# Where weight parts start within 256 bytes: all of them at 64 or 192, and the tiles behind the sinks' 128 bytes further on

## The chip, the cores and the metric

The kernel runs on one core of one Trainium2 chip. The metric is device time in microseconds (us) of one execution. The kernel before took 1211.8 us, the median of 3 runs (1211.75 to 1212.57).

TensorE (PE in the profile, PEld for its weight loads) multiplies; VectorE (DVE) and ScalarE (ACT) do the elementwise work; GpSimd (POOL) does a little; SyncE (SP) issues most DMAs. SBUF is the memory on the chip that all of them read: 128 partitions, and in each of them a tile has a start address in bytes. "Place" in this document is that address modulo 256.

## What is computed

Two layers of a decoder trunk on 512 tokens of width 1024, in float32. Cut to the parts that matter here:

```python
for i in range(DEPTH):                                  # 2 layers
    h = _rms_norm(x, mix_norm[i])
    if i % 2 == 0:                                      # sliding-window attention and short convolution
        x = x + _attn_conv_mixer(h, cos, sin, hy_w_in[j], ..., hy_sinks[j], ..., hy_w_out[j])
    else:                                               # chunked gated linear attention
        x = x + _gla_mixer(h, gla_w_in[j], ..., gla_w_out[j])
    x = x + _conv_ffn(_rms_norm(x, ffn_norm[i]), ffn_w_up[i], ..., ffn_w_down[i])
    x = x + _per_layer_embedding(x, p[i], ple_norm[i], ple_w_gate[i], ple_w_proj[i])
```

Nearly all the arithmetic is in the products with the weights: `hy_w_in`, `hy_w_out`, `gla_w_in`, `gla_w_out`, `ple_w_gate`, `ple_w_proj`, and above all `ffn_w_up` (1024 x 5632) and `ffn_w_down` (2816 x 1024).

## The kernel before

**Split products.** A float32 value is cut into a high part, which ScalarE rounds to the type float32r, and a low part, which VectorE gets as the difference. A product of two such values is three matmuls: high x high, high x low, low x high (`mm3`, lines 162 to 168; the third line of the three, L168, has the low part of the stationary side). Weights arrive by DMA in tiles "raw" and are cut into tiles "wh" and "wl"; activations are cut into pairs "a", "b" (normed activations), "uh" and "ul" (the feed-forward's inner values), "yh" and "yl" (the mixers' outputs), "ph" and "pl" (the embedding).

**Two ways to cut weights.** `cut` makes plain parts; they serve `mm3`, mostly as the stationary operand (128 x 128), with 512 tokens moving. `cut_blocks` and `first_forms` make parts for `seven` (lines 875 to 877), which computes a 2 x 2 block product with seven products instead of eight; there 256 tokens move. The sums of activations that the seven products need lie in tiles "four" (and low parts beside them). `seven` serves the feed-forward's gate columns in the up-projection and some of the down-projection. In it `product` issues 4 x 3 = 12 matmuls: of the seven products, four have "four" as their moving side and three have plain activations. In `down` the rows of inner values come in sets A (8 to 13), B (0 to 7) and C (14 to 21); A and C are cut into "four" tiles, B into uh and ul.

**Roles.** In a few places the weights are the moving side and the activations the stationary one: the keys, values and queries of the first mixer, the values of the second, and the gate of the last embedding (`ple1`, lines 1372 to 1374 by its helper `add`). That gate also has some weight chunks in "four" tiles rather than wh and wl.

**Where tiles lie.** Tiles stand in pools, and a pool gives each tag its buffers one after the other, in the order of first use. The pools are laid out in this order: constants (cp), the residual (xp), activations a and b (fp), weights raw, wh, wl (wp), scratch (sp), small columns (sm), and behind them the pool of the running stage, which holds "four", the inputs, the attention's and the linear attention's tiles, "zt" and "z". Sizes up to the small columns are multiples of 256 bytes, so a, b, raw, wh and wl start at place 0. Tiles of wh and wl are 1088 elements wide (4352 bytes, 17 x 256), of which 1024 are used; `weight_tiles` says from which element on. `cut` takes element 0; `cut_blocks` and `first_forms` pass BLOCKS = (16, 48), so that wh starts 64 bytes and wl 192 bytes behind the tile's start. The small columns are 32 bytes each; among them is "sink", 16 elements (64 bytes). They end at place 128, and so all the tiles of the stage pools start at place 128.

**Order.** TensorE's order in the heavy stages is the program's (a manual schedule); the change leaves every engine's instructions in the order that they had.

Of the kernel before, what the change touches and what calls it, by code (L numbers as in the profile page):

```python
# [9 lines left out]
F32 = mybir.dt.float32  # L10
F32R = mybir.dt.float32r
# [7 lines left out]
P = 128  # L19
S = 512  # L20
# [6 lines left out]
NQ, NKV, HD = 8, 2, 64  # L27
# [27 lines left out]

BLOCKS = (16, 48)


class Kernel:
# [53 lines left out]
        self.nc.sync.dma_start(raw, src)  # L115
        return self.cut(raw, by)

    def weight_tiles(self, offs=(0, 0)):

        return [  # L120
            self.wp.tile([P, 1024 + 64], F32R, tag=g, name=self.nm(g), bufs=3)[:, o : o + 1024]
            for g, o in zip(("wh", "wl"), offs)
        ]

    def raw(self, na, nb):
# [303 lines left out]
    def mixer0(self):  # L429
        nc, a, tc = self.nc, self.a, self.tc  # L430
        with tc.tile_pool(name="m0", bufs=1) as mp:
# [62 lines left out]
            self.end_norm(sums=sums)  # L494
            with tc.issue_after(last[1].ins):
                C, Sn = self.rope_tables(mp)
            sink = self.sm.tile([P, 16], F32, name="sink", bufs=1)[:, :NQ]
            self.late(sink[:, :1])
            nc.gpsimd.dma_start(sink, a["hy_sinks"][0:1, :].partition_broadcast(P))
            nc.vector.tensor_scalar_mul(sink, sink, -1.0)  # L500
            h = HD // 2
# [310 lines left out]
    def cut_blocks(self, src, wide=True):  # L812

        nc = self.nc
        if wide:
            h, l = self.weight_tiles(BLOCKS)
        else:
            h, l = (
                self.sp.tile([P, S + 64], F32R, tag="sq", name=self.nm("t2"), bufs=2)[:, o : o + S] for o in BLOCKS
            )  # L820
        h, l = (x.rearrange("p (j n) -> p j n", n=src.shape[2]) for x in (h, l))
        nc.scalar.activation(h, src, AF.Copy)  # L822
        nc.vector.tensor_tensor(l, src, h.bitcast(F32), ALU.subtract)  # L823
        h, l = (x.rearrange("p j n -> p (j n)").rearrange("p (k n) -> p k n", n=P) for x in (h, l))
        n = 2 if wide else 1
        return lambda j, c: (h[:, n * j + c, :], l[:, n * j + c, :])
# [7 lines left out]
    def first_forms(self, ev, od, raw=None):  # L834

        nc = self.nc
        b11, b12, b21, b22 = ev[:, :, :P], ev[:, :, P:], od[:, :, :P], od[:, :, P:]
        if raw is not None:
            plain = self.cut_blocks(raw[:, :, :P])
        else:  # L840
            h, l = self.weight_tiles(BLOCKS)
            h, l = (x.rearrange("p (j u n) -> p j u n", u=2, n=P) for x in (h, l))
            for u, b in enumerate((b11, b21)):
                self.split((h[:, :, u], l[:, :, u]), b)
            plain = lambda j, c: (h[:, j, c], l[:, j, c])
        nc.vector.tensor_tensor(b11, b12, b11, ALU.subtract)
        nc.vector.tensor_tensor(b12, b22, b12, ALU.subtract)  # L847
        return plain
# [242 lines left out]
    def down(self, i, acts, forms, both, work, finish):  # L1091
# [76 lines left out]
        for t, p in enumerate(plan):  # L1168
            todo.append((1, lambda t=t: cut(t)))
            if p[4] is not None:  # L1170
                todo.append((1, lambda u=p[4]: first_forms(u)))
                todo.append((1, lambda u=p[4]: more_forms(u)))
# [804 lines left out]
```

## Time and profile before

| what | value |
| --- | --- |
| median of the runs | 1211.8 us (1211.75 to 1212.57) |
| the profiled execution, whole | 1211.79 us |
| its span in the profile | 1210.0 us |
| granted TensorE clock | 1.0 |
| instructions | 17728, of them 7018 matmuls and 7018 weight loads |
| HBM traffic | 114.37 MB read, 2.10 MB written |

How to read it: the page gives the busy time of each engine and its share of the span. A group of instructions has the line of the kernel, the engine, the operation, then output<-inputs by tile names, the shapes, the count, the busy time and the mean duration of one in ns. The timeline lists instructions by start time (first column, us) and duration (second column, us). Matmuls are pipelined: one starts well before the one ahead of it has ended, so the distance of two starts, not the duration, is what a matmul costs. The profile has no addresses; they come from the built program.

### The profile page before, as it was taken

How to read it: one execution, taken by the hardware profiler on the slowest of the kernel's cores; microseconds unless marked ns; L12 is line 12 of the kernel's file. 1: busy time of each engine (PE TensorE's matmuls, PEld its weight loads, DVE VectorE, ACT ScalarE, POOL GpSimd, SP SyncE). 2: the span in 40 equal slices, each digit the busy share in tenths (PEclk: the TensorE clock that was granted, in tenths of full speed). 3: DMA queues.
4: the chain of work that ended last, by engine and by line, in shares of the span. 5: the costliest groups of instructions: out<-in, count | busy, mean ns of one | idle time of the engine just before them, and what ended most of it. 6: DMA issues, size and time to landing. Idle time of an engine off the chain costs nothing.

```text
span 1210.0 us, 17728 instructions
## 1 busy us (share of the span) xinstructions
PE 1203.6 (99%) x7018; PEld 1042.1 (86%) x7018; DVE 969.4 (80%) x1543; ACT 667.9 (55%) x1093; POOL 44.7 (4%) x64
## 2 busy tenths in 40 slices
PE   9999999999999999999999999999999999999998
PEld 8877789999999889888988988889999999888887
DVE  6786687899989986746679876778999898978595
ACT  7466565656554643534563654555665555645374
POOL 2600000000000000000100000000000000000000
PEclk9999999999999999999999999999999999999999
DMA  7232222324242332232322212322232423322501
GB/s 221 76 101 70 73 70 77 133 71 139 71 139 70 127 114 86 92 105 80 111 93 69 77 64 71 104 87 88 88 123 70 140 70 131 122 87 100 206 1 70
DMA packets 111128, 117.61 MB, mean 97 GB/s; under 512 B 2841, under 2 KB 106323, under 8 KB 111045
## 3 DMA queue, kind: packets, MB, share of 16 engines
q1 hardware_dynamic: 109680, 115.35, 28.8%
q8 instruction: 55, 0.90, 0.3%
q0 software_dynamic: 560, 0.42, 0.2%
q10 hardware_dynamic: 804, 0.70, 0.2%
q14 instruction: 29, 0.23, 0.1%
HBM read 114.37 MB, written 2.10 MB: 96 GB/s over the span
## 4 chain that ended last, share of the span: by engine, by line
PE 95%; DVE 3%; ACT 1%; issue 0%; ACTq 0%
PE ps L166 14%; PE ps L167 14%; PE ps L168 14%; PE pa L167 7%; PE pa L166 7%; PE pa L168 7%; PE ps L875 6%; PE ps L876 6%; PE ps L877 6%; PE pa L875 2%; PE pa L876 2%; PE pa L877 2%; PE ps L1374 1%; PE ps L1373 1%; PE ps L1372 1%; DVE wl L147 1%
## 5 line engine op out<-in xcount | busy, mean ns | idle before, releaser
L146 ACT ACTIVATE wh<-raw 128x1024 fp32r<-128x1024 f32 (+4 forms) x154 | 152.4, 992 | 150.4 <-PE ps L167 103.2
L147 DVE TENSOR_TENSOR wl<-raw,wh 128x1024 fp32r<-128x1024 f32 (+4 forms) x154 | 175.1, 1138 | 56.4 <-ACT wh L146 55.6
L822 ACT ACTIVATE wh<-raw 128x1024 fp32r<-128x1024 f32 x78 | 82.7, 1061 | 124.0 <-DVE raw L847 65.8
L935 DVE SCALAR_TENSOR_TENSOR zt<-z,vfa,zt 128x510 f32<-128x510 f32 (+1 forms) x176 | 130.6, 744 | 11.7 <-ACT zt L933 11.2
L823 DVE TENSOR_TENSOR wl<-raw,wh 128x1024 fp32r<-128x1024 f32 x78 | 95.3, 1222 | 20.6 <-ACT wh L822 20.5
L933 ACT ACTIVATE zt<-z,vfb 128x512 f32<-128x512 f32 x88 | 71.0, 809 | 23.9 <-DVE four L986 12.8
L166 PE MATMUL ps<-b,wh 128*128 128x512 f32 x192 | 76.6, 399 | 0.0
L167 PE MATMUL ps<-b,wh 128*128 128x512 f32 x192 | 75.1, 391 | 0.0
L168 PE MATMUL ps<-b,wl 128*128 128x512 f32 x192 | 74.9, 390 | 0.0
L167 PE MATMUL pa<-a,wh 128*128 128x512 f32 x176 | 69.1, 392 | 0.0
L167 PE MATMUL pa<-b,wh 128*128 128x512 f32 x176 | 69.0, 392 | 0.0
L166 PE MATMUL pa<-a,wh 128*128 128x512 f32 x176 | 68.8, 391 | 0.0
L166 PE MATMUL pa<-b,wh 128*128 128x512 f32 x176 | 68.8, 391 | 0.0
L168 PE MATMUL pa<-a,wl 128*128 128x512 f32 x176 | 68.7, 390 | 0.0
L168 PE MATMUL pa<-b,wl 128*128 128x512 f32 x176 | 68.6, 390 | 0.0
L876 PE MATMUL ps<-four,wh 128*128 128x256 f32 x232 | 65.3, 281 | 0.0
L875 PE MATMUL ps<-four,wh 128*128 128x256 f32 x232 | 65.1, 281 | 0.0
L877 PE MATMUL ps<-four,wl 128*128 128x256 f32 x232 | 64.8, 279 | 0.0
L166 PE MATMUL ps<-a,wh 128*128 128x512 f32 x160 | 63.6, 398 | 0.0
L167 PE MATMUL ps<-a,wh 128*128 128x512 f32 x160 | 62.4, 390 | 0.0
L168 PE MATMUL ps<-a,wl 128*128 128x512 f32 x160 | 62.4, 390 | 0.0
L166 PE MATMUL ps<-uh,wh 128*128 128x512 f32 x128 | 50.2, 392 | 0.0
(472 smaller groups left out, 3500.6 us busy)
## 6 DMA issues: line engine op xcount, KB each, us to landing
raw<-in_ffn_w_up_dram SPq DMA_DIRECT2D x44, 1024.0 KB, 5.0
raw<-in_ffn_w_down_dram SPq DMA_DIRECT2D x13, 1024.0 KB, 4.7
raw<-in_hy_w_in_dram SPq DMA_DIRECT2D x8, 1024.0 KB, 4.9
raw<-in_gla_w_in_dram SPq DMA_DIRECT2D x8, 1024.0 KB, 5.0
raw<-in_ffn_w_down_dram SPq DMA_DIRECT2D x8, 768.0 KB, 4.1
raw<-in_ple_w_gate_dram SPq DMA_DIRECT2D x6, 1024.0 KB, 4.6
raw<-in_hy_w_out_dram SPq DMA_DIRECT2D x16, 256.0 KB, 4.0
raw<-in_gla_w_out_dram SPq DMA_DIRECT2D x4, 1024.0 KB, 4.6
```

Source lines behind the costliest of these rows:

```text
L146: nc.scalar.activation(hv, v, AF.Copy)
L147: nc.vector.tensor_tensor(lv, v, hv.bitcast(F32), ALU.subtract)
L166: mm(out, lh, rh, start=start, stop=False, **kw)
L167: mm(out, lh, rl, start=False, stop=False, **kw)
L168: mm(out, ll, rh, start=False, stop=stop, **kw)
L822: nc.scalar.activation(h, src, AF.Copy)
L823: nc.vector.tensor_tensor(l, src, h.bitcast(F32), ALU.subtract)
L875: mm(out, wh, xh, start=first and j == 0, stop=False, **kw)
L876: mm(out, wh, xl, start=False, stop=False, **kw)
L877: mm(out, wl, xh, start=False, stop=j == ND // 2 - 1, **kw)
L933: nc.scalar.activation(y, z, AF.Identity, scale=w2[:, f : f + 1], bias=bb[:, f : f + 1])
L935: nc.vector.scalar_tensor_tensor(out=y[:, tap:], in0=z[:, : S - tap], scalar=w[:, f : f + 1], in1=y[:, tap:], op0=ALU.mult, op1=ALU.add,)
```

## The change

Every pair of weight tiles now starts at elements (16, 48), those of `cut` and of `ple1` too; the constant has a new name and `weight_tiles` no argument. The tile "sink" is 48 elements wide instead of 16, of which the same 8 are used, so the small columns behind it and all tiles of the stage pools move by 128 bytes: the latter from place 128 to place 0. The tiles of a, b, u, y and raw stay where they were. No instruction is added, removed or moved, and no shape changes.

```diff
-BLOCKS = (16, 48)
+STARTS = (16, 48)
...
-    def weight_tiles(self, offs=(0, 0)):
+    def weight_tiles(self):
 
         return [
             self.wp.tile([P, 1024 + 64], F32R, tag=g, name=self.nm(g), bufs=3)[:, o : o + 1024]
-            for g, o in zip(("wh", "wl"), offs)
+            for g, o in zip(("wh", "wl"), STARTS)
         ]
...
-            sink = self.sm.tile([P, 16], F32, name="sink", bufs=1)[:, :NQ]
+            sink = self.sm.tile([P, 48], F32, name="sink", bufs=1)[:, :NQ]
...
         if wide:
-            h, l = self.weight_tiles(BLOCKS)
+            h, l = self.weight_tiles()
         else:
             h, l = (
-                self.sp.tile([P, S + 64], F32R, tag="sq", name=self.nm("t2"), bufs=2)[:, o : o + S] for o in BLOCKS
+                self.sp.tile([P, S + 64], F32R, tag="sq", name=self.nm("t2"), bufs=2)[:, o : o + S] for o in STARTS
             )
...
-            h, l = self.weight_tiles(BLOCKS)
+            h, l = self.weight_tiles()
```

## The prediction

> **What bounds the kernel now.** I read the page first, then the waits of TensorE, then its groups with shapes kept apart, and last the timeline of single matmuls, because the change alters no instruction, only where tiles lie.
>
> ```profile
> span 1210.0 us, 17728 instructions
> ...
> PE 1203.6 (99%) x7018; PEld 1042.1 (86%) x7018; DVE 969.4 (80%) x1543; ACT 667.9 (55%) x1093; POOL 44.7 (4%) x64
> ...
> PEclk9999999999999999999999999999999999999999
> ...
> PE 95%; DVE 3%; ACT 1%; issue 0%; ACTq 0%
> ```
>
> TensorE is busy in 1203.6 of 1210.0 us, at the full granted clock, and holds 95% of the chain that ended last. The longest of its waits is only
>
> ```profile
> PE pa L201 <- DVE mhalf L190: 1.3, 1, 1.3
> ```
>
> So the time is the number of matmuls times their pitch, the time from one matmul's start to the next one's. Anything the change does must show in that pitch. The busy means (390, 281 ns) are no pitch, since pipelined matmuls overlap; starts in the timeline give it.
>
> **The pitch by place.** A place below is an address modulo 256 bytes. In the built program before the change, the plain activations (a, b, uh, ul, yh, yl) lie at 0, the tile "four" (with its neighbours behind the sinks' tile) at 128, the parts wh and wl from `cut` at 0, and those from `cut_blocks` and `first_forms` at 64 and 192. Write "moving/weights". Two 256-wide products with block weights stand side by side late in the second down-projection, each of 4 block rows x 3 matmuls = 12:
>
> ```profile
> 1084.51 0.28 PE L875 MATMUL pa<-b,wh 128*128 128x256 f32 x1
> ...
> 1085.87 0.28 PE L875 MATMUL ps<-four,wh 128*128 128x256 f32 x1
> ...
> 1087.30 0.28 PE L875 MATMUL ps<-b,t 128*128 128x256 f32 x1
> ...
> 1099.91 0.28 PE L875 MATMUL pa<-b,wh 128*128 128x256 f32 x1
> ...
> 1101.29 0.28 PE L875 MATMUL ps<-four,wh 128*128 128x256 f32 x1
> ```
>
> With moving b (0/64 and 192): 1.36 us / 12 = 113.3 ns, and in the later pair 1.38 / 12 = 115.0. With moving four (128/64 and 192): 1.43 / 12 = 119.2 ns. Nothing else differs: same lines, shape and weight places. The 512-wide matmuls show it as well, in the last column pair of that stage (8 row blocks x 2 columns x 3 = 48, then 14 x 2 x 3 = 84):
>
> ```profile
> 1119.64 0.39 PE L166 MATMUL ps<-uh,wh 128*128 128x512 f32 x1
> ...
> 1130.54 0.40 PE L166 MATMUL ps<-four,wh 128*128 128x512 f32 x1
> ...
> 1150.13 0.39 PE L1372 MATMUL ps<-wh,b 128*128 128x512 f32 x1
> ```
>
> uh and ul (0/0): 10.90 / 48 = 227.1 ns. four (128/0): 19.59 / 84 = 233.2 ns. And the weights' place counts, not the moving operand's alone: in the second embedding gate, where four is the stationary side (0/128), and in the key and value products at the start (0/0, but 256 wide):
>
> ```profile
> 1183.08 0.39 PE L167 MATMUL pa<-wl,four 128*128 128x512 f32 x1
> ...
> 1185.65 0.40 PE L1372 MATMUL ps<-four,a 128*128 128x512 f32 x1
> ```
>
> ```profile
> 17.22 0.28 PE L166 MATMUL pa<-wh,a 128*128 128x256 f32 x1
> ...
> 22.86 0.28 PE L168 MATMUL pa<-wh,a 128*128 128x256 f32 x1
> ```
>
> The first is 11 matmuls from the second of twelve to the end, 2.57 / 11 = 233.6 ns; the other 47 steps (4 row blocks x 4 token tiles x 3, less one), 5.64 / 47 = 120.0 ns. So there is a floor, 113.3 ns for 256 columns and 2 x 113.3 = 226.6 for 512, and a lock about 6.5 ns above it, which some pairs of places fall into and stay in. Known at the floor: 512 wide 0/0; 256 wide 0/64,192. Known above it: 512 wide 128/0 and 0/128; 256 wide 128/64,192 and 0/0. **Not in the trace: 512 wide with 0/64,192**, which is just what the change makes of most matmuls.
>
> **The change, part by part.** Instruction order is the same on every engine, so I price places alone.
>
> ```profile
> L168 PE MATMUL ps<-b,wl 128*128 128x512 f32 x192 | 74.9, 390 | 0.0
> L167 PE MATMUL pa<-a,wh 128*128 128x512 f32 x176 | 69.1, 392 | 0.0
> ...
> L168 PE MATMUL pa<-b,wl 128*128 128x512 f32 x176 | 68.6, 390 | 0.0
> ...
> L877 PE MATMUL ps<-four,wl 128*128 128x256 f32 x232 | 64.8, 279 | 0.0
> ...
> L168 PE MATMUL ps<-a,wl 128*128 128x512 f32 x160 | 62.4, 390 | 0.0
> ...
> L168 PE MATMUL ps<-uh,wl 128*128 128x512 f32 x128 | 49.9, 390 | 0.0
> L168 PE MATMUL ps<-four,wl 128*128 128x512 f32 x112 | 44.2, 395 | 0.0
> ...
> L877 PE MATMUL pa<-four,wl 128*128 128x256 f32 x116 | 32.3, 278 | 0.0
> ...
> L877 PE MATMUL ps<-b,wl 128*128 128x256 f32 x112 | 31.1, 278 | 0.0
> ...
> L168 PE MATMUL ps<-yh,wl 128*128 128x512 f32 x64 | 24.9, 389 | 0.0
> ...
> L877 PE MATMUL ps<-four,t 128*128 128x256 f32 x88 | 24.6, 280 | 0.0
> ...
> L168 PE MATMUL ps<-wh,b 128*128 128x336 f32 x64 | 20.3, 317 | 0.0
> ...
> L168 PE MATMUL ps<-wh,a 128*128 128x512 f32 x32 | 12.5, 389 | 0.0
> ...
> L168 PE MATMUL ps<-wh,b 128*128 128x368 f32 x32 | 10.4, 329 | 0.0
> ...
> L168 PE MATMUL pa<-wh,a 128*128 128x256 f32 x32 | 9.0, 282 | 0.0
> ...
> L168 PE MATMUL ps<-ph,wl 128*128 128x512 f32 x16 | 6.3, 395 | 0.0
> ...
> L1374 PE MATMUL ps<-four,a 128*128 128x512 f32 x14 | 5.5, 395 | 0.0
> ...
> L1374 PE MATMUL ps<-four,b 128*128 128x512 f32 x12 | 4.7, 395 | 0.0
> ```
>
> Each row is one of the three matmuls of a split product, so counts go times 3.
>
> 1. *four under block weights*, 3 x (232 + 116 + 88) = 1308 matmuls, 128/64,192 to 0/64,192: both ends are in the trace, 119.2 to 115.0 ns (the slower of the two b runs): 1308 x 4.2 = 5.5 us gained. Bounds: 7.7 with 113.3; about 2 by the busy means alone (279 or 280 on four against 278 on b, 1 to 2 ns). I take 5.5, the nearest rows.
>
> 2. *four and ph under plain weights*, 3 x (112 + 16) = 384, 128/0 to 0/64,192. If this place sits at the floor, 384 x (233.2 - 227.1) = 2.3 us; if not, 0.
>
> 3. *Plain weights under a, b, u, y*, 3 x (192 + 176 + 176 + 160 + 128 + 64) = 2688, 0/0 to 0/64,192. They have the floor already and can't gain there. What they can gain is relocking: their busy mean is 390 to 392 ns where yh, an undisturbed stretch, has 389. The same product of b costs 115.0 ns at 1099.91 but 113.3 at 1084.51, so after a switch of places some slow matmuls seem to pass before the floor is found. About 2 ns x 2688 = 5.4 us goes so; afterwards weights keep one pair of places and only widths switch, so I take half, 2.7 us (bounds 0 and 5.4). The loss that could stand here is rival two.
>
> 4. *four over activations in the second gate*, 3 x (14 + 12) = 78, 128/0 to 0/0: 78 x 6.1 = 0.5 us, both ends in the trace.
>
> 5. *Weights as the moving side* (rows with wh ahead of a or b: 3 x 32 key and value matmuls, 3 x 32 of the queries, 3 x (64 + 32) of the second mixer's values, and the second gate's own) now start at 64 or 192. At 120.0 ns the first are above the floor, the second at it; one lock either way on some 270 of them is 270 x 6.1 = 1.6 us, up or down. I take 0.
>
> 6. *ScalarE and VectorE* write the parts at other places. The same split exists at both:
>
> ```profile
> L147 DVE TENSOR_TENSOR wl<-raw,wh 128x1024 fp32r<-128x1024 f32 x119 | 145.2, 1221 | 47.5 <-ACT wh L146 46.7
> L823 DVE TENSOR_TENSOR wl<-raw,wh 128x1024 fp32r<-128x1024 f32 x78 | 95.3, 1222 | 20.6 <-ACT wh L822 20.5
> ```
>
> 1221 against 1222 ns: nothing. VectorE could become the bound in the first steps of each up-projection, where it is nearly full:
>
> ```profile
> 840.00:880.00 40.00, 40.00 (x258) 36.30 (x257) 39.08 (x54) 24.33 (x37) 0.00 (x0) 1.00 0.28 91
> ```
>
> (columns: span, then busy and count of PE, PEld, DVE, ACT, POOL). DVE has 39.08 of 40 us. Four such steps per layer, each with 4 products x 12 matmuls on four: 8 x 48 x 4.2 = 1.6 us of part 1 could be kept back there. I keep that for the range.
>
> Sum: 5.5 + 2.3 + 2.7 + 0.5 = 11.0 us off a span of 1210.0, 1199.0; the profiled execution took 1211.79 in all, 1.8 more than its span and equal to the median of 1211.8. Forecast **1200.8 us**.
>
> One rule speaks against all this. The Trainium skill, "TensorE: Matmul & The Clock Gate", section on the steps of a matmul, has two independent read ports into the array, so that loading the next weights takes no read bandwidth from the running matmul; its page "SBUF — State Buffer", section "Who interferes with whom", says "PE and ACT never wait on anyone." By these a tile's place would be worth nothing and the sum would be 0. The trace disagrees: 113.3 against 119.2 ns for one operation.
>
> **The rivals.** *One: places decide nothing* (the 119.2 belongs to tiles high in memory or to what runs beside them), and the change only moves addresses: 1211.8. For it: four is always both at 128 and high, so the rows can't separate these. Against: wh over four at 0/128 pays the same 6 ns with the high tile on the other side, and the key products pay it with no high tile at all. *Two, slower: the 512-wide matmuls lock high at 0/64,192.* Then the 2688 of part 3 go from about 227.1 + 2 to 233.2, +4.1 each, 11.0 us lost; part 2 gains nothing, the relocking gain is gone, parts 1 and 4 still give 6.0: +5.0, so 1216.8 us; with no relocking cost today it would be 2688 x 6.1 - 6.0 = +10.4. It decides as soon as the 512-wide ones settle more than 6.0 us / 2688 = 2.2 ns above today's mean of 229, at 231. For it: 0/0 is good at 512 and bad at 256, so what is good at 256 needn't be good at 512; and 0/128 is bad. Against: no row with moving at 0 and weights at 64 or 192 is locked high. *Three: only part 1 and part 4 pay*, the rest even: 1205.8, inside the forecast's side.
>
> **How the numbers follow.** Forecast and rival three 0.58 together (0.50 and 0.08), rival one 0.08, rival two 0.34. The likeliest one's own range is 1195 (7.7 + 2.3 + 5.4 + 0.5 + 1.6 of part 5 is 17.5, less what switching widths will keep) to 1206. Rival two holds more than the 2 in 10 that may be left out, so the range goes over its price: **1195 to 1219**. A difference of 0.2% (2.4 us) is about what a measurement of this kernel tells from none. Faster 0.58, within it 0.08, slower 0.34.
>
> **What would show it.** In the profile after: the starts of L875 with four, 12 per product, at 113 to 115 ns (part 1; at 119 it is wrong); L166 to L168 with uh or yh, 48 in 10.9 us (floor) or 11.2 us (rival two), and their busy mean 389 or 395; the run of 84 over four at 19.1 us instead of 19.59 (part 2); means of a and b rows moving towards 389 (part 3); L147 and L823 unchanged; DVE as releaser of TensorE in the first up-projection steps if part 6 bites. If the 512-wide pitch stands above 231 ns in the long runs, the forecast is wrong however well the rest went.

## The result, and the profile after

| | before | changed |
| --- | --- | --- |
| median | 1211.7 us (1210.91 to 1212.57, 10 runs) | 1215.17 us (1214.45 to 1215.78, 10 runs) |
| span of the profiled execution | 1210.0 us | 1212.7 us |

The ratio is 1.0027, with a 95% interval of 1.0018 to 1.0037: the change costs 3.5 us. The forecast was 1200.8 us; rival two (1216.8) is the one that came about.

First the page of the changed kernel: span, engines, clock, and the chain that ended last by engine.

```profile
span 1212.7 us, 17728 instructions
...
PE 1206.3 (99%) x7018; PEld 1036.7 (85%) x7018; DVE 969.4 (80%) x1543; ACT 667.2 (55%) x1093; POOL 45.2 (4%) x64
...
PEclk9999999999999999999999999999999999999999
...
PE 97%; DVE 2%; DMA 0%; ACT 0%; issue 0%; SPq 0%; DVEq 0%
```

TensorE's busy time rose by 2.7 us, as the span did, at the same clock and with the same instructions. VectorE and ScalarE stand where they were. TensorE's longest wait is also the old one, as its view of waits shows (total, times, longest, us):

```profile
PE pa L201 <- DVE mhalf L190: 1.3, 1, 1.3
```

So the loss is pitch, not waiting. The groups, shapes kept apart (count, busy us, mean ns of one, idle ahead), say which matmuls:

```profile
L168 PE MATMUL ps<-b,wl 128*128 128x512 f32 x192 | 76.2, 397 | 0.0
...
L168 PE MATMUL ps<-uh,wl 128*128 128x512 f32 x128 | 50.7, 396 | 0.0
...
L877 PE MATMUL pa<-four,wl 128*128 128x256 f32 x116 | 32.2, 277 | 0.0
...
L168 PE MATMUL ps<-yh,wl 128*128 128x512 f32 x64 | 25.4, 397 | 0.0
```

On L168, yh, the undisturbed stretch at the floor before with 389 ns, has 397 now, and b and uh went from 390 to 397 and 396. All L168 rows of a, b, u and y rose by 6 to 8 ns, their L166 and L167 rows by at most 4; the 256-wide row fell by 1. The timeline (start, duration, us) gives the pitch, at the places that the prediction used:

```profile
1102.97 0.28 PE L875 MATMUL pa<-b,wh 128*128 128x256 f32 x1
...
1104.34 0.28 PE L875 MATMUL ps<-four,wh 128*128 128x256 f32 x1
...
1105.70 0.28 PE L875 MATMUL ps<-b,t 128*128 128x256 f32 x1
...
1122.53 0.39 PE L166 MATMUL ps<-uh,wh 128*128 128x512 f32 x1
...
1133.66 0.39 PE L166 MATMUL ps<-four,wh 128*128 128x512 f32 x1
...
1153.13 0.39 PE L1372 MATMUL ps<-wh,b 128*128 128x512 f32 x1
...
1188.59 0.39 PE L1372 MATMUL ps<-four,a 128*128 128x512 f32 x1
...
1191.99 0.39 PE L1372 MATMUL ps<-four,b 128*128 128x512 f32 x1
```

The block product on four takes 1.36 / 12 = 113.3 ns (119.2 before): the floor. The last column pair of the second down-projection, 48 matmuls on uh and ul and then 84 on four, takes 11.13 / 48 = 231.9 and 19.47 / 84 = 231.8 ns, where it had 227.1 and 233.2. In the second gate four under activations, now 0/0, runs at 3.40 / 15 = 226.7.

To see what each part is worth over the whole run, I joined the timeline's matmuls with the built program's addresses and summed, for all matmuls with the same kind of operands, the time from each one's start to the next start:

| matmuls | count | before, us | after, us | difference | predicted |
| --- | --- | --- | --- | --- | --- |
| blocks on four (part 1) | 1308 | 155.15 | 151.26 | -3.9 | -5.5 |
| plain on four and ph (part 2) | 384 | 89.50 | 89.02 | -0.5 | -2.3 |
| plain on a, b, u, y (part 3) | 2688 | 619.51 | 628.63 | +9.1 | -2.7 |
| second gate, four moving (part 4) | 78 | 18.25 | 17.83 | -0.4 | -0.5 |
| weights moving, 512 and 336 wide (most of part 5) | 366 | 70.97 | 71.10 | +0.1 | 0 |
| blocks on a and b | 1128 | 130.16 | 129.17 | -1.0 | not priced |

The rows sum to 3.4 us; the remaining matmuls, most of them small, give 0.7 back, which makes the 2.7 of the span. One row decides: 2688 matmuls at +3.4 ns each.

### The profile page after: what moved, and what is told of

Same layout as the page of the kernel before. It is cut to its first block, busy times and chain, and to the rows that moved or that the text cites. A ratio compares the mean times of both kernels' runs of the same rounds, so it can differ in the third digit from the quotient of the medians.

```text
span 1212.7 us, 17728 instructions
## 1 busy us (share of the span) xinstructions
PE 1206.3 (99%) x7018; PEld 1036.7 (85%) x7018; DVE 969.4 (80%) x1543; ACT 667.2 (55%) x1093; POOL 45.2 (4%) x64
## 4 chain that ended last, share of the span: by engine, by line
PE 97%; DVE 2%; DMA 0%; ACT 0%; issue 0%; SPq 0%; DVEq 0%
PE ps L166 15%; PE ps L168 15%; PE ps L167 15%; PE pa L168 7%; PE pa L167 7%; PE pa L166 7%; PE ps L875 6%; PE ps L877 5%; PE ps L876 5%; PE pa L875 2%; PE pa L876 2%; PE pa L877 2%; PE pa L1690 1%; PE ps L1374 1%; PE pa L1810 1%; PE ps L1372 1%
## 5 line engine op out<-in xcount | busy, mean ns | idle before, releaser
L166 PE MATMUL ps<-b,wh 128*128 128x512 f32 x192 | 77.2, 402 | 0.0
L168 PE MATMUL ps<-b,wl 128*128 128x512 f32 x192 | 76.2, 397 | 0.0
L167 PE MATMUL ps<-b,wh 128*128 128x512 f32 x192 | 75.6, 394 | 0.0
L168 PE MATMUL pa<-a,wl 128*128 128x512 f32 x176 | 69.7, 396 | 0.0
L168 PE MATMUL pa<-b,wl 128*128 128x512 f32 x176 | 69.7, 396 | 0.0
L167 PE MATMUL pa<-a,wh 128*128 128x512 f32 x176 | 69.0, 392 | 0.0
L167 PE MATMUL pa<-b,wh 128*128 128x512 f32 x176 | 69.0, 392 | 0.0
L166 PE MATMUL pa<-a,wh 128*128 128x512 f32 x176 | 69.0, 392 | 0.0
L166 PE MATMUL pa<-b,wh 128*128 128x512 f32 x176 | 69.0, 392 | 0.0
L166 PE MATMUL ps<-a,wh 128*128 128x512 f32 x160 | 64.1, 401 | 0.0
L168 PE MATMUL ps<-a,wl 128*128 128x512 f32 x160 | 63.4, 396 | 0.0
L167 PE MATMUL ps<-a,wh 128*128 128x512 f32 x160 | 62.7, 392 | 0.0
L168 PE MATMUL ps<-uh,wl 128*128 128x512 f32 x128 | 50.7, 396 | 0.0
```

Source lines behind the costliest of these rows:

```text
L166: mm(out, lh, rh, start=start, stop=False, **kw)
L167: mm(out, lh, rl, start=False, stop=False, **kw)
L168: mm(out, ll, rh, start=False, stop=stop, **kw)
```

## Experiments

In each, only the lines shown or named differ from the kernel before. The pitch is read at the same two stretches throughout: the 48 + 84 = 132 matmuls of the last column pair (512 wide; uh, ul and four are all at place 0 wherever the sink is 48 wide, and at 64 in the kernel that moves everything by 64), and a stretch of three block products, 36 matmuls (256 wide, on b, four, b). Where a kernel was timed once, the kernel before is beside it from the same chip.

**The sink's width alone.** Plain parts stay at 0, four goes from 128 to 0.

```diff
-            sink = self.sm.tile([P, 16], F32, name="sink", bufs=1)[:, :NQ]
+            sink = self.sm.tile([P, 48], F32, name="sink", bufs=1)[:, :NQ]
```

> Only the tiles behind the sinks' move by 128 bytes (four to place 0); plain weight parts stay at 0, block parts at 64 and 192. Theory (the loss is the 512-wide matmuls at 0/64,192, pitch 231.9 against 227.1 ns, and the moved tiles are a gain): the 1308 block matmuls on four go from 118.6 to about 114.4 ns, 5.5 us gained, the 462 512-wide ones on four from 233.3 to about 227.1, 2.9 us gained: 1203.3 us. Rival A (the moved tiles themselves cost, through the other engines or through relocking between places): at or above the time before, 1212 to 1216 us.

Measured: 1204.53 us (1204.09 to 1205.48, 4 runs) against 1211.52 (7 runs), ratio 0.9943 [0.9928, 0.9958]. Its timeline:

```profile
1093.66 0.28 PE L875 MATMUL pa<-b,wh 128*128 128x256 f32 x1
...
1097.77 0.40 PE L166 MATMUL ps<-uh,wh 128*128 128x512 f32 x1
...
1113.08 0.39 PE L166 MATMUL ps<-uh,wh 128*128 128x512 f32 x1
...
1143.00 0.39 PE L1372 MATMUL ps<-wh,b 128*128 128x512 f32 x1
```

29.92 / 132 = 226.7 ns, the floor on uh and on four, and 4.11 / 36 = 114.2 for the blocks. Summed over the run as above, part 1 gives 4.5 us, part 2 the full 2.3, part 4 0.5; part 3 comes out 1.0 dearer. So half of the change is a gain of 7.0 us.

**The plain parts alone.** The other half: the sink stays 16 wide, so four stays at 128.

```diff
-    def weight_tiles(self, offs=(0, 0)):
+    def weight_tiles(self, offs=(16, 48)):
```

> Only the plain weight parts move to 64 and 192; four stays at 128. Theory: the 2688 matmuls on a, b, u and y go to a pitch of about 231.9 ns from a mean of 228.5, 9 us lost, and the 384 on four (128/64,192 at 512 wide, in no trace yet) lie between 227 and 233: 1218 to 1221 us. Rival A (the plain parts are innocent): 1209 to 1212 us.

Measured: 1217.73 us (1217.11 to 1218.34, 4 runs), ratio 1.0050 [1.0033, 1.0067], just under the range that the theory gave. Timeline:

```profile
1048.75 0.39 PE L166 MATMUL ps<-four,wh 128*128 128x512 f32 x1
...
1065.23 0.39 PE L166 MATMUL ps<-uh,wh 128*128 128x512 f32 x1
...
1125.76 0.39 PE L166 MATMUL ps<-uh,wh 128*128 128x512 f32 x1
...
1136.88 0.39 PE L166 MATMUL ps<-four,wh 128*128 128x512 f32 x1
...
1156.48 0.39 PE L1372 MATMUL ps<-wh,b 128*128 128x512 f32 x1
```

uh at 0/64,192 has 11.12 / 48 = 231.7 ns, as in the changed kernel, and part 3 summed over the run is 8.7 us dearer than before: this half carries the loss. The four rows are a surprise: 84 matmuls at 19.60 / 84 = 233.3 ns, and 72 others in a row, with the same places, at 16.48 / 72 = 228.9. The two halves, -7.0 and +6.2, do not add up to +3.5. The sums by part say why: four under plain weights gains 2.3 us with the sink alone and 0.8 with the plain parts alone, but 0.5 with both (2.6 short of the sum), and the blocks on four 4.5 and 1.4 alone, but 3.9 with both (2.0 short).

**Both plain parts at one place, 64 or 192.** Does the price lie in one of the two places, or in the jump between high and low part? Both with the wide sink:

```diff
-    def weight_tiles(self, offs=(0, 0)):
+    def weight_tiles(self, offs=(16, 16)):
...
-            sink = self.sm.tile([P, 16], F32, name="sink", bufs=1)[:, :NQ]
+            sink = self.sm.tile([P, 48], F32, name="sink", bufs=1)[:, :NQ]
```

> The changed kernel with both plain parts at 64 (block parts still at 64 and 192). Theory B (a place of 64 under moving 0 is above the floor whatever the other part's place): long runs of 512-wide matmuls stay near 232 ns, time 1213 to 1217 us. Rival C (it is the jump from 64 to 192 inside a split product that costs): long runs at 226.7 to 227.1 ns, and with 3072 of them 5 ns cheaper about 1200 us.

Measured: 1216.38 us, against 1211.52. Timeline, with the 96 query matmuls of the first mixer ahead (512 wide), where the weights are the moving side:

```profile
22.82 0.50 PE L166 MATMUL ps<-wh,a 128*128 128x512 f32 x1
...
44.93 0.49 PE L525 MATMUL pa<-cf,kn 128*128 128x128 f32 x3
...
1124.21 0.39 PE L166 MATMUL ps<-uh,wh 128*128 128x512 f32 x1
...
1155.01 0.39 PE L1372 MATMUL ps<-wh,b 128*128 128x512 f32 x1
```

0/64: 30.80 / 132 = 233.3 ns, with no jump in it at all. So the jump isn't the cause. Weights moving, 64/0: 22.11 / 96 = 230.3 (228.3 with the sink alone, 0/0, on the same stretch).

The same with (48, 48):

> The changed kernel with both plain parts at 192. Theory B: near 232 ns, or, if 64 and 192 are not equal, a pitch of its own between 226.7 and 237 ns, since in the changed kernel the steps from a part at 192 to one at 64 had the longest distances (233 to 238 ns) and those among 64 the shorter (229 to 233). Rival C: 226.7 to 227.1 ns, about 1200 us.

Measured: 1210.61 us. Timeline, same stretches:

```profile
23.20 0.50 PE L166 MATMUL ps<-wh,a 128*128 128x512 f32 x1
...
45.71 0.49 PE L525 MATMUL pa<-cf,kn 128*128 128x128 f32 x3
...
1118.77 0.39 PE L166 MATMUL ps<-uh,wh 128*128 128x512 f32 x1
...
1148.98 0.39 PE L1372 MATMUL ps<-wh,b 128*128 128x512 f32 x1
```

0/192: 30.21 / 132 = 228.9 ns. Weights moving, 192/0: 22.51 / 96 = 234.5. Read together: 0/64 costs 6.6 over the floor and 0/192 2.2; with the roles turned round, 64/0 costs 2.0 and 192/0 6.2. The two agree if what counts is the **distance**, stationary start minus moving start modulo 256: a distance of 64 is dear in both, one of 192 cheap in both. They agree to the tenth once the first ten of the 96, slow in every kernel, and the last are left out: the steps from start to start then average 226.7 ns at 0/0, 228.9 at 64/0 and 233.3 at 192/0. And of the three matmuls of a split product two have the high part as the stationary side (distance 64) and one the low part (192): (2 x 233.3 + 228.9) / 3 = 231.8 ns, the mean that the changed kernel has. Its single steps are not these two values, though: from L166, L167 and L168 to the next start they average 231.1, 228.9 and 235.5 ns over 192 matmuls in a row.

**All tiles 64 bytes further on, distances kept.** If only the distance counts, this must give the time of the sink alone.

```diff
-        self.mhalf = self.cp.tile([P, 32], F32, name="mhalf")[:, :16]
+        self.mhalf = self.cp.tile([P, 48], F32, name="mhalf")[:, :16]
...
-            sink = self.sm.tile([P, 16], F32, name="sink", bufs=1)[:, :NQ]
+            sink = self.sm.tile([P, 48], F32, name="sink", bufs=1)[:, :NQ]
```

> The kernel of the first experiment (sinks' tile 48 wide, plain parts at the tiles' start) with 64 more bytes in the constants ahead of everything, so that activations, weights and stage tiles all lie 64 bytes further on and their distances stay. Theory D (what counts is the weights' place less the moving side's, modulo 256): time and pitches of the first experiment, 1204.5 us, long 512-wide runs at 226.8 to 227.2 ns. Rival E (the weights' own place counts: 64 cost 6.7 ns where the moving side lay at 0): long runs at 230 to 233 ns or more, some 3000 x 5 ns, 1217 to 1222 us.

Measured: 1205.90 us, against 1211.39. Timeline:

```profile
1114.77 0.39 PE L166 MATMUL ps<-uh,wh 128*128 128x512 f32 x1
...
1144.69 0.39 PE L1372 MATMUL ps<-wh,b 128*128 128x512 f32 x1
```

29.92 / 132 = 226.7: the floor, at 64/64. Between 0 and 64, then, the place in itself makes no difference here, and the distance does. The time is 1.4 us above that of the sink alone, from one run.

**The blocks' distances.** Four kernels with the wide sink, and for the block parts (0, 0), (64, 64), (192, 192) and (192, 64) bytes in place of (64, 192); for the first:

```diff
-BLOCKS = (16, 48)
+BLOCKS = (0, 0)
```

> The first experiment's kernel with the block parts at 0 as well, so that every weight part lies at 0 and every activation too. Theory from the key and value products (256 wide at 0/0, 120.0 ns): the 2436 block matmuls go from a mean of 115.0 to 120.0 ns, 12.2 us lost, less some 6 us of relocking between widths that falls away: 1210 to 1217 us. Rival F (the key products are slow for another reason, and 0/0 is as good at 256 as at 512): pitch 113.3 to 114 ns, 1196 to 1200 us.

Measured: 1215.41 us, against 1211.39. Timeline:

```profile
1104.73 0.28 PE L875 MATMUL pa<-b,wh 128*128 128x256 f32 x1
...
1109.04 0.40 PE L166 MATMUL ps<-uh,wh 128*128 128x512 f32 x1
```

4.31 / 36 = 119.7 ns: at 256 columns distance 0 is the dear one, though at 512 it is the floor.

> The first experiment's kernel with both block parts at 64. If the place of one part alone sets the block matmuls' pitch, 256 wide at distance 64 is at the floor (113.3 ns) and the time stays at 1200 to 1205 us, the lower end if fewer slow matmuls follow a change of width; if the mixture of 64 and 192 is needed, block pitches of 117 to 120 ns and 1209 to 1217 us.

Measured: 1211.11 us, against 1211.39. Timeline:

```profile
1100.50 0.28 PE L875 MATMUL pa<-b,wh 128*128 128x256 f32 x1
...
1104.74 0.40 PE L166 MATMUL ps<-uh,wh 128*128 128x512 f32 x1
```

4.24 / 36 = 117.8 ns. Each kernel has 87 block products that do not open a stretch (an unbroken row of block matmuls), and 83 of them stand there; the other four are at 113.3. So a distance of 64 throughout seldom reaches the floor, where the pair (64, 192) has it nearly always (86 of 87 with the sink alone).

> The same with both block parts at 192. A distance of 192 costs 2.3 ns at 512 columns; if the price at 256 columns is alike, 2436 x 2.3 = 5.6 us more than the first experiment, 1210 us; if 192 is at the floor at 256 columns, 1200 to 1205 us.

Measured: 1208.79 us, against 1211.39, between the times that the theories gave. Timeline, two stretches of 36 with the same operands in the same order:

```profile
1082.78 0.28 PE L875 MATMUL pa<-b,wh 128*128 128x256 f32 x1
...
1086.86 0.40 PE L166 MATMUL ps<-uh,wh 128*128 128x512 f32 x1
...
1098.21 0.28 PE L875 MATMUL pa<-b,wh 128*128 128x256 f32 x1
...
1102.45 0.40 PE L166 MATMUL ps<-uh,wh 128*128 128x512 f32 x1
```

4.08 / 36 = 113.3 and 4.24 / 36 = 117.8 ns: two levels at one and the same distance, 15 us apart. The upper one is the rule, 82 of the 87. Against the sink alone the block matmuls take 7.0 us more and the 2688 of part 3 take 2.9 less, most of it in the first ones behind a change of width; that puts the time between those of the theories.

> The first experiment's kernel with the block parts swapped: high parts at 192, low parts at 64. By Theory D this has the distances that block weights at 64 and 192 had under four at 128 in the kernel before (192, 192, 64), where 256 columns cost 118.6 to 119.2 ns: 2436 x 4 = 9.7 us over the first experiment, 1212 to 1215 us. Rival G (only the mixture counts, not which part has which place): floor, 1202 to 1206 us.

Measured: 1203.61 us, against 1211.73. Timeline:

```profile
466.92 0.39 PE L875 MATMUL ps<-a,wh 128*128 128x256 f32 x1
467.14 0.28 PE L876 MATMUL ps<-a,wh 128*128 128x256 f32 x1
...
468.44 0.28 PE L875 MATMUL ps<-four,wh 128*128 128x256 f32 x1
...
469.87 0.39 PE L166 MATMUL ps<-uh,wh 128*128 128x512 f32 x1
...
1093.18 0.28 PE L875 MATMUL pa<-b,wh 128*128 128x256 f32 x1
...
1097.27 0.40 PE L166 MATMUL ps<-uh,wh 128*128 128x512 f32 x1
```

4.09 / 36 = 113.6 ns: the floor, where 77 of the 87 block products stand. The distances here are 192, 192, 64 in the three matmuls, and those of four in the kernel before (128/64,192) are the same, and stood at 119.2. So at 256 columns the distance alone doesn't give the pitch: the expectation drawn from it missed. This kernel has the upper level too: the product at 468.44 takes 1.43 / 12 = 119.2 ns, and eight of the 87 stand at 119. All eight lie behind a late start in the same stretch, a matmul that begins 159 to 226 ns after the one before it (here 220 ns, at 467.14); four more behind such a start stay at the floor, and no product without one is in the upper level. Addresses don't choose: each pair of full start addresses in the eight also occurs in products at the floor. One run doesn't separate this kernel from the sink alone.

**The plain parts the other way round.** By distance, (192, 64) should have the cheap distance twice: (2 x 228.9 + 233.3) / 3 = 230.4 ns.

```diff
-    def weight_tiles(self, offs=(0, 0)):
+    def weight_tiles(self, offs=(48, 16)):
...
-            sink = self.sm.tile([P, 16], F32, name="sink", bufs=1)[:, :NQ]
+            sink = self.sm.tile([P, 48], F32, name="sink", bufs=1)[:, :NQ]
```

> The changed kernel with the plain parts swapped: high at 192, low at 64. If the prices at 512 columns add up by part (64: 6.7 ns, 192: 2.3 ns, as the runs with both parts at one place gave), the mean is (2 x 2.3 + 6.7) / 3 = 3.8 ns over the floor, 230.4 to 230.5 ns in long runs against 231.9 in the changed kernel: 3072 x 1.4 = 4.4 us less than it, 1209 to 1212 us. If the order of parts counts at 512 as it may at 256, another pitch, below 229 or above 232.

Measured: 1218.32 us, against 1211.73, the slowest of all. Timeline:

```profile
1126.01 0.40 PE L166 MATMUL ps<-uh,wh 128*128 128x512 f32 x1
...
1156.81 0.39 PE L1372 MATMUL ps<-wh,b 128*128 128x512 f32 x1
```

30.80 / 132 = 233.3 ns, as if all three were at 64. In another long stretch of this kernel, 282 matmuls from 746.67 to 811.31 us, it is 229.2, as if all were at 192. The mean of 230.4 was seen in no long stretch: this order takes one of two levels, as four did with the plain parts alone, where the distances are the same. So the prices do not add up by part, and that their sum gave the changed kernel's 231.8 may be chance.

**Blocks at 0 and 128, two orders**, with the wide sink, in search of a pair that gains more:

```diff
-BLOCKS = (16, 48)
+BLOCKS = (0, 32)
```

> The first experiment's kernel with the block parts at 0 and 128, looking for a mixture that is at the floor and needs less relocking after a change of width (the first experiment spends about 116 x 27 + 112 x 15 ns = 4.8 us so). Floor and less relocking: 1200 to 1204 us. If 0 costs 6.7 ns in a mixture as it did alone at 256 columns: 1208 to 1215 us.

Measured: 1214.24 us, against 1211.73.

> The same with the parts swapped, 128 and 0. Same two cases: 1200 to 1204 us, or 1208 to 1215 us with block pitches of 117 to 120 ns.

Measured, with (32, 0): 1212.97 us. The stretch of 36 block matmuls takes 4.27 us in both, 118.6 ns each. Both lose what the wide sink gains, and a little more.

## Why the prediction was wrong

**The bound** was right: no wait and no other engine came in. TensorE's busy time and the span moved by the same 2.7 us.

**The step that failed** is part 3, with the condition that part 2 hung on. It put 512-wide matmuls with 0/64,192, the one pair that the trace of before did not have, at the floor, because the 256-wide ones have it there. The runs show that the two widths go by different prices: distance 0 is the floor at 512 (226.7) and the dearest seen at 256 (119.7), and the pair of 64 and 192 is the floor at 256 (113.3) and 5.1 ns above it at 512 (231.8). The argument that "no row with moving at 0 and weights at 64 or 192 is locked high" rested on 256-wide rows only; the row beside it, 0/0 good at 512 and bad at 256, had already shown that one width doesn't speak for the other.

**Part 3's size.** It was to gain 2.7 us and lost 9.1. The relocking that it hoped to save was not saved. Six matmuls on uh and ul between the same two block products take 1.39 us in the kernel before,

```profile
1104.08 0.40 PE L166 MATMUL ps<-uh,wh 128*128 128x512 f32 x1
...
1105.47 0.28 PE L875 MATMUL ps<-b,wh 128*128 128x256 f32 x1
```

and 1.39 us in the changed one:

```profile
1107.06 0.39 PE L166 MATMUL ps<-uh,wh 128*128 128x512 f32 x1
...
1108.45 0.28 PE L875 MATMUL ps<-b,wh 128*128 128x256 f32 x1
```

In the 68 stretches of twelve or more 512-wide matmuls right behind 256-wide ones, the first eight take 1840 ns before and 1846 after (medians). So the slow start lasts as long as it did; it only stands less above a settled pitch that is higher. The mean of the 2688 is 3.8 ns above the settled pitch before (619.51 us / 2688 = 230.5 against 226.7) and 2.1 in the changed kernel (233.9 against 231.8).

**Part 2** was to gain 2.3 us and gained 0.5: four went from 233.2 to 231.8 instead of 227.1. With plain parts at 0 the full 2.3 came, so the price of the step was right and its "if" wrong.

**Part 1** was right in mechanism, 119.2 to 113.3 in the runs quoted; summed it gave 3.9 of 5.5 us, since the mean over all 1308 was 118.6 before, not 119.2, and 115.6 after: the first matmuls after a switch are slow still. **Part 4** gave 0.4 of 0.5. **Part 5** came to 0.1 in the 366 matmuls counted, of an assumed 0. **Part 6** held: no new wait on VectorE in the first up-projection steps.

**Rival two** had the place and the direction right and the size nearly: it set the 512-wide ones to 233.2 and got 1216.8 us; they settled at 231.8, above its point of decision at 231. That its sum came so near is in part luck: it had part 3 1.9 us too dear, and parts 1 and 4 together 1.7 us too good. The range reached to 1219 only for this rival's sake; the forecast's own ended at 1206. Rival one, that places decide nothing, is refuted by the sink alone: 7.0 us from addresses.

What stays open: by what mechanism the distance sets the pitch, and why one set of distances can stand at two levels (113.3 or 117.8 and 113.3 or 119 at 256 columns; 228.9 or 233.3 at 512). Both occur within one execution and at the same addresses. In two kernels the rarer level comes only behind a late start (all eight products with the blocks at 192 and 64, all four with both at 64), which points to what ran just before; with both at 192 only one of five does, and no run changed the starts on purpose.

## What to carry to other kernels

Where TensorE is full and nothing waits, read the pitch from start to start for each width and each pair of start addresses, and let no width stand in for another: a pair that the trace doesn't show is an experiment, not a term of a sum. Here the best is distance 0 modulo 256 for 512-wide matmuls and the parts at 64 and 192 for 256-wide ones, which is the wide sink alone, the fastest of the kernels timed more than once: 1204.53 us, 0.9943 [0.9928, 0.9958] of the time before. A change that treats both alike should be taken apart before it is judged, since one half can hide the other's gain.

## What was not expected of the hardware

The pitch of a 512-wide float32r matmul goes by the distance of its two operands' starts modulo 256 bytes: 226.7 ns at 0 (at 0/0 and at 64/64), 233.3 at 64, 233.2 at 128 (128/0), 228.9 at 192. These are for three matmuls of a split product at one distance. So the sign of the distance matters, 64 costing three times what 192 does, and it costs with either operand as the moving one. The Trainium skill's page "TensorE: Matmul & The Clock Gate", section on the steps of a matmul, gives the array separate ports for the moving data and for the weights; from this it concludes that loading the next weights takes no read bandwidth from the running matmul. The runs disagree in so far as the pitch of the two together hangs on the distance of their addresses, by up to 6.6 ns; by what mechanism they don't show. The order of two places matters too: plain parts at (64, 192) gave 231.8 ns in the last column pair, at (192, 64) 233.3, and the latter elsewhere 229.2. At 256 columns the prices are others: 119.7 ns at distance 0, mostly 117.8 at 64 or at 192 alone, and 113.3 to 113.6 for the two mixed, from a moving side at place 0.
